# A fixed TensorE order in the attention, scores and weights of exactly 128 columns, and two query blocks' scores in one PSUM bank

## The chip, the core and the metric

The kernel runs on one core of a Trainium2 chip. A core has a matrix engine (TensorE, PE in the profile; its weight loads are listed as PEld), a vector engine (VectorE, DVE), a scalar engine (ScalarE, ACT), a general engine (GpSimd, POOL) and a queue engine that here starts the loads (SyncE, SP). Each engine works through its own queue in order, and an instruction waits on semaphores that other engines raise. TensorE writes its results to PSUM, a small memory of eight banks, each of which holds 512 float32 columns on 128 partitions; the other engines read them there.

The metric is the device time of one execution in microseconds (us). The kernel before was run three times, 884.99, 886.83 and 887.63 us, with the median 886.83.

## The reference

One block of a streaming encoder, for 512 frames of 1024 features, in float32:

```python
xn = rmsnorm(h, norm_mix_g[l])
u = jnp.einsum('bsd,de->bse', xn, w_in[l])
q, k, v, xr, gr, ga, gb = jnp.split(u, splits, axis=-1)
ya = chunked_band_attention(q, k, v, rel_table[l]) @ w_attn_out[l]
...
h = h + (g_a * ya + g_b * yb) @ w_o[l]
...
h = h + (jax.nn.silu(g) * up) @ w_ffn_out[l]
```

The second branch `yb` is a causal convolution, a gated linear recurrence and a projection. The attention is what the change touches. It has 16 heads of 64 features. Frames lie in chunks of 64; a frame reads its own chunk and the eight chunks before it, and since there are only eight chunks, that is every chunk up to its own. A learned bias by clipped distance is added to the scores, then softmax, then the weighted sum of the values:

```python
s = jnp.einsum('bnqhd,bnkhd->bhnqk', q, kb).astype(jnp.float32) * scale
s = s + rel_bias_band(rel_table).astype(jnp.float32)[None, :, None, :, :]
...
p = jax.nn.softmax(s, axis=-1).astype(v.dtype)
o = jnp.einsum('bhnqk,bnkhd->bnqhd', p, vb)
```

## The kernel before

**Numbers in two parts.** Every float32 operand of a matmul is split into a high part, rounded to the type `float32r`, and the rest. ACT makes the high part and DVE the rest (`split`, lines 78 to 81). A full product takes three matmuls (`mm3`, lines 74 to 76): high by high, high by low, low by high. Weights arrive by loads on SP's queue (line 149), 512 KB at a time, and are split before use; in the profile these tiles are called `raw_..` and `whl_..`.

**Stages.** Norm and transposes, then the projections of the recurrent branch with its scan, then the attention, then the output projections (`ya`, `wo`), and the feed-forward part. In the time line the attention stands between about 235 and 448 us.

**The attention.** For a pair of heads `q_tile` and `k_tile` make q and k by 24 matmuls of 512 columns each, and evict them with ACT and DVE; `v_tile` makes a block of v for four heads with 24 matmuls of 256 columns. One head then has four steps.

- `scores(h)`, lines 638 to 659: the 512 queries are four blocks of 128. Query block `qb` reads the first `(qb + 1) * 128` keys. Two matmuls (lines 651 and 652) make its scores; both parts of q lie in one stationary operand, against the high and the low part of k. The matmuls are never under 256 columns wide: block 0 computes 256 and uses 128. The scores of blocks 0, 1 and 3 go to a PSUM tag `s` of two banks, those of block 2 to a tag `mm` of four. DVE adds the bias and finds the row's maximum in one instruction, followed by a short read-out into `m` (both at line 654); ACT takes the exponential and the row sum (line 655); DVE makes the reciprocals of the sums (line 656); POOL scales the four blocks (line 658). The bias tile of the head is loaded by SP and masked by POOL (lines 424 and 425).
- `transposed(h)`, lines 661 to 673: ten transposes on PE (line 670) turn the probabilities so that keys lie on partitions. Three PSUM tiles receive them, and ACT and DVE split them into tiles `pp`. The third `pp` holds key blocks 2 and 3; key block 3 has only 128 columns of queries, and 128 columns of zeros are set before it by POOL (line 664), so that its part is 256 wide. It is split in two pieces, of 256 and 128 columns.
- `weigh(h)`, lines 679 to 698: eight matmuls (line 690) of 512, 512, 384, 384, 256, 256, 256 and 256 columns add up the weighted values in one PSUM tile, which ACT and DVE evict.
- `laid(h)`, lines 702 to 711, names the projections that are put into the turn of head `h`, before or after its weighing: q and k tiles of later pairs, v blocks of the next group, and for heads 12 to 15 a gate projection each. Turns 4, 8 and 12 to 15 have one tile of 512 columns and nothing else.

**What sets the order.** The program is written out in the turns of lines 722 to 731: the transposes of head `h`, the scores of head `h + 1`, the projections before, the weighing, the projections after. The scores of head 0 are made earlier, among the projections `yb` (line 718). But the written order is not the order of the engines: the kernel is built with a scheduler (line 984) that puts the instructions of each engine into an order of its own, by a simulated time line. In the order it made, the scores of a head are often parted, with the fourth or third block many matmuls behind the others, and a weighing is mixed with scores or transposes of other heads. Waits are then set between the engines, where one instruction reads what another wrote or writes where another still reads.

Of the kernel before, what the change touches and what calls it, by code (L numbers as in the profile page):

```python
# [8 lines left out]
F32 = mybir.dt.float32  # L9
# [5 lines left out]
P = 128  # L15
D = 1024
S = 512
KT = D // P
NT = S // P
HEADS = 16  # L20
# [16 lines left out]
def block_kernel(ctx: ExitStack, tc: tile.TileContext, x, norm_mix_g, w_in, b_merge, rel_table,  # L37
# [3 lines left out]
    pe, dve, act, pool, sp = nc.tensor, nc.vector, nc.scalar, nc.gpsimd, nc.sync  # L41
# [21 lines left out]
    ps = ctx.enter_context(tc.tile_pool(name="ps", bufs=2, space=PSUM))  # L63
    dr = ctx.enter_context(tc.tile_pool(name="dr", bufs=1, space=bass.MemoryType.DRAM))

    def f(ap):
        return ap.bitcast(F32)

    def mm_tile(name, tag="mm"):
        return ps.tile([P, S], F32, tag=tag, bufs=4 if tag == "mm" else 2, name=name)  # L70
# [7 lines left out]
    def split(hi, lo, src):  # L78

        act.activation(hi, src, AF.Copy)  # L80
        dve.tensor_sub(lo, src, f(hi))  # L81
# [280 lines left out]
    def features(pl, tag, name):  # L362

        t = pl.tile([P, KT, 2, S], F32R, tag=tag, name=name)
        return t, [t[:, k] for k in range(KT)]
# [13 lines left out]
    _, xnT = features(xnp, "xn", "xnT")  # L379
# [40 lines left out]
    def bias_tile(h):  # L420
        b = aw.tile([P, S], F32, tag="bias", bufs=2, name=f"bias{h}")
        src = ext_d[h:h + 1, 0:S]
        band = bass.AP(tensor=src.tensor, offset=src.offset, ap=[[1, P], [1, S]])
        sp.dma_start(out=b[:], in_=band)
        pool.memset(b[64:128, 448:512], NEG)
        return b
# [150 lines left out]
    def blocks(ap):  # L577
        return ap.rearrange("p (b i) -> p b i", i=P)

    def backwards(ap):  # L580
        return blocks(ap)[:, :, ::-1]

    def halves(e):
        own, other = slice(e * HD, e * HD + HD), slice(HD - e * HD, 2 * HD - e * HD)
        return own, other
# [7 lines left out]
    def q_tile(pr):  # L593
        po = mm_tile(f"po_q{pr}")
        project(po, weights(f"qk{pr}"), 0, xnT)
        q = qk_pool(pr).tile([P, 2, S], F32R, tag="qk", bufs=3, name=f"q{pr}")
        for e in range(2):
            own, other = halves(e)
            src = backwards(po[own, :])
            act.activation(blocks(q[own, e]), src, AF.Copy, scale=0.125)  # L600
            dve.scalar_tensor_tensor(blocks(q[other, e]), src, 0.125, blocks(f(q[own, e])), ALU.mult, ALU.subtract)
        qk[pr] = [q]

    def k_tile(pr):
        po = mm_tile(f"po_k{pr}")
        project(po, weights(f"qk{pr}"), 1, xnT)
        kh = qk_pool(pr).tile([P, 2, S], F32R, tag="qk", bufs=3, name=f"kh{pr}")
        kl = qk_pool(pr).tile([P, 2, S], F32R, tag="qk", bufs=3, name=f"kl{pr}")
        for e in range(2):
            own, other = halves(e)  # L610
            act.activation(kh[own, e], po[own, :], AF.Copy)
            dve.tensor_sub(kl[own, e], po[own, :], f(kh[own, e]))
            act.activation(kh[other, e], po[own, :], AF.Copy)
            pool.tensor_copy(kl[other, e], kl[own, e])
        qk[pr] += [kh, kl]
# [11 lines left out]
    def v_tile(gr, t):  # L627
        wv = weights(f"v{gr}")
        po = mm_tile(f"po_v{gr}_{t}", "mm" if gr else "t")
        for k in range(KT):  # L630
            mm3(po[:, 0:256], xnT[k][:, 0, t * P:(t + 1) * P], xnT[k][:, 1, t * P:(t + 1) * P],
                wv(0, k, whole), wv(1, k, whole), k == 0, k == KT - 1)
        v = aw.tile([P, 2, 4, HD], F32R, tag="v", bufs=8, name=f"v{gr}_{t}")
        split(v[:, :, 0::3], v[:, :, 1:3], po[:, 0:256].rearrange("p (a b d) -> p a b d", a=2, b=2))
        vs.setdefault(gr, []).append(v)


    def scores(h):
        pr, e = divmod(h, 2)
        q, kh, kl = qk[pr]  # L640
        bias = bias_tile(h)
        lsum = cp.tile([P, NT], F32, tag="lsum", bufs=2, name=f"l{h}")
        nmax = cp.tile([P, NT], F32, tag="nmax", bufs=2, name=f"m{h}")
        rl = cp.tile([P, NT], F32, tag="rl", bufs=2, name=f"rl{h}")
        prob = [aw2.tile([P, (qb + 1) * P], F32, tag=f"p{qb}", name=f"p{h}_{qb}") for qb in range(NT)]
        for qb in range(NT):
            w = (qb + 1) * P
            wm = max(w, 256)
            sc = mm_tile(f"s{h}_{qb}") if qb == 2 else ps.tile([P, S], F32, tag="s", bufs=2, name=f"s{h}_{qb}")
            qs = q[:, e, qb * P:(qb + 1) * P]  # L650
            pe.matmul(sc[:, 0:wm], qs, kh[:, e, 0:wm], start=True, stop=False)
            pe.matmul(sc[:, 0:wm], qs, kl[:, e, 0:wm], start=False, stop=True)  # L652

            dve.tensor_tensor_reduce(prob[qb][:], sc[:, 0:w], bias[:, S - w:S], -1.0, 3e38, ALU.add, ALU.min, nmax[:, qb:qb + 1])  # L654
            act.activation(prob[qb][:], prob[qb][:], AF.Exp, bias=nmax[:, qb:qb + 1], scale=-1.0, accum_out=lsum[:, qb:qb + 1])  # L655
        dve.reciprocal(rl[:], lsum[:])  # L656
        for qb in range(NT):
            pool.tensor_scalar(prob[qb][:], prob[qb][:], rl[:, qb:qb + 1], 1.0, ALU.mult, ALU.mult)  # L658
        return prob

    def transposed(h, prob):

        pp = [aw2.tile([P, 2, S], F32R, tag="pt", bufs=4, name=f"pp{h}_{i}") for i in range(3)]
        pool.memset(f(pp[2][:, :, 256:384]), 0.0)
        for i, kbs in enumerate(((0,), (1,), (2, 3))):
            pt = mm_tile(f"pT{h}_{i}") if i == 2 else ps.tile([P, S], F32, tag="t", bufs=2, name=f"pT{h}_{i}")
            for kb in kbs:
                for qb in range(kb, NT):
                    at = qb - min(kb, 2) if kb < 3 else 2
                    pe.transpose(pt[:, at * P:(at + 1) * P], prob[qb][:, kb * P:(kb + 1) * P], ident[:])  # L670
            for at, lo, n in (((0, 0, 512),), ((0, 0, 384),), ((0, 0, 256), (384, 256, 128)))[i]:
                split(pp[i][:, 0, at:at + n], pp[i][:, 1, at:at + n], pt[:, lo:lo + n])
        return pp

    aT = []
# [3 lines left out]
    def weigh(h, pp):  # L679
        pr, e = divmod(h, 2)  # L680
        own, other = halves(e)
        if e == 0:
            oacc.append(tg_.tile([P, S], F32, tag="tg", name=f"oacc{pr}"))
        acc = oacc[pr]
        po = mm_tile(f"o{h}")
        for kb in range(NT):
            i, lo, n = ((0, 0, 512), (1, 0, 384), (2, 0, 256), (2, 256, 256))[kb]
            st = vs[pr // 2][kb][:, pr % 2, 2 * e:2 * e + 2].rearrange("p a d -> p (a d)")
            for part in range(2):
                pe.matmul(po[:, S - n:S], st, pp[i][:, part, lo:lo + n], start=kb == 0 and part == 0, stop=kb == NT - 1 and part == 1)  # L690
        act.activation(acc[own, :], po[other, :], AF.Copy)
        dve.tensor_add(acc[own, :], po[own, :], acc[own, :])
        if e == 1:
            if pr % 2 == 0:
                aT_pairs.append(rnp.tile([P, 2, 2, S], F32R, tag="big", bufs=4, name=f"aT{pr}"))
            o = aT_pairs[-1][:, pr % 2]
            split(blocks(o[:, 0]), blocks(o[:, 1]), backwards(acc[:]))
            aT.append(o)
# [3 lines left out]
    def laid(h):  # L702
        m, at = divmod(h, 4)
        qs, ks, va = (lambda pr: lambda: q_tile(pr)), (lambda pr: lambda: k_tile(pr)), (lambda t: lambda: v_tile(m + 1, t))
        if h >= 12:
            return [lambda: gate(0, h - 8)], []
        first_, second = 2 * m + 2, 2 * m + 3
        return {0: (([qs(1), ks(1)] if m == 0 else []) + ([] if m == 0 else [qs(first_)]), [qs(first_)] if m == 0 else []),
                1: ([ks(first_)], [va(0)]),
                2: ([va(1), va(2)], [va(3)]),  # L710
                3: ([qs(second)], [ks(second)])}[at]
# [4 lines left out]
    for j in range(KT):  # L716
        if j == 6:
            prob = scores(0)
        po = mm_tile(f"po_yb{j}")
        project(po, weights(f"yb{j - j % 2}"), j % 2, rnn)  # L720
        dve.scalar_tensor_tensor(zB[j], zB[j], 1.0, po[:], ALU.add, ALU.mult)
    for h in range(HEADS):
        pp = transposed(h, prob)
        if h + 1 < HEADS:
            prob = scores(h + 1)
        before, after = laid(h)
        for what in before:
            what()
        weigh(h, pp)
        for what in after:  # L730
            what()
    aw2_stack.close()
    wo_stack, wop = opened("wo", 4)
    extra["wo1"] = wop
# [3 lines left out]
    _, mT = features(xnp, "xn", "mT")  # L738
# [113 lines left out]
    sc_stack, sc = opened("sc", 2)  # L852
# [101 lines left out]
    for i, ((t, at), po) in enumerate(zip(pieces, pos)):  # L954
        for k0, wf in zip(ks[late:], wfs):
            out_tile(t, po, k0, wf, at)
        n = 1 + i // 4
# [30 lines left out]
```

## Time and profile before

| | |
|---|---|
| median of three runs | 886.83 us |
| the profiled execution's own time | 887.36 us |
| its span, first to last instruction | 885.6 us |
| mean granted TensorE clock | 0.997 |
| TensorE busy | 873.6 us, 99% of the span |
| weight loads busy | 778.1 us, 88% |
| DVE busy | 551.7 us, 62% |
| ACT busy | 472.6 us, 53% |
| POOL busy | 111.4 us, 13% |

The busy time of PE is that of overlapping matmuls: a matmul's record reaches past the start of the next one. What a matmul costs in a row of matmuls is therefore read from start to start, not from its length. The profile's other views are groups of instructions (line, engine, operation, written tile <- read tiles, shapes, count, then busy time and mean length in ns of one, then the idle time of the engine ahead of them and who ended it), the waits (who waited for whom: us in total, times, the longest), the time line (start, length, engine, line, operation, and in brackets the idle time before it), and the busy time of each engine by stretch with the granted clock.

### The profile page before, as it was taken

The page shows a single profiled execution, that of the slowest core. Times are in us where ns is not written, and L with a number is a line of the kernel's source. Part 1 is how long each engine was busy: PE and PEld are TensorE (multiplying, and loading weights), DVE is VectorE, ACT ScalarE, POOL GpSimd, SP SyncE. Part 2 cuts the span into 40 slices and gives each one's busy share as a digit, 9 for nine tenths or more (in the row PEclk, how much of TensorE's full clock was granted, in tenths as well). Part 3 has the DMA queues.
Part 4 walks back from the last instruction along what each step waited for, and adds up shares of the span by engine and source line. Part 5 has one row for each costly group of instructions (what it writes and reads, how often), then busy time and mean ns, then how long its engine had stood idle before and what let it go on. Part 6 is the DMA issues. An engine that isn't in the chain of part 4 may idle for free.

```text
span 885.6 us, 13331 instructions
## 1 busy us (share of the span) xinstructions
PE 873.6 (99%) x5220; PEld 778.1 (88%) x5220; DVE 551.7 (62%) x872; ACT 472.6 (53%) x839; POOL 111.4 (13%) x157
## 2 busy tenths in 40 slices
PE   8999999999999999999999999999999999999997
PEld 5988888888888989898888889999999999888886
DVE  5776557663456475765556556888878887553203
ACT  7566646652256485766633366656555555723203
POOL 4013111220022232222100000000000001300100
PEclk9999999999999999999999999999999999999999
DMA  8223233433333233232223720524333332353002
GB/s 266 86 82 104 86 95 94 122 95 95 97 96 93 61 96 96 72 108 72 62 84 121 258 75 22 165 74 126 113 95 96 100 128 84 119 180 126 27 1 95
DMA packets 86080, 90.10 MB, mean 102 GB/s; under 512 B 5377, under 2 KB 74609, under 8 KB 86017
## 3 DMA queue, kind: packets, MB, share of 16 engines
q1 hardware_dynamic: 84640, 85.78, 31.6%
q10 hardware_dynamic: 1376, 3.47, 1.0%
q8 instruction: 41, 0.67, 0.3%
q14 instruction: 23, 0.18, 0.1%
HBM read 87.10 MB, written 2.14 MB: 101 GB/s over the span
## 4 chain that ended last, share of the span: by engine, by line
PE 96%; DVE 2%; DMA 1%; ACT 1%; issue 0%; POOL 0%; ACTq 0%; DVEq 0%
PE po_out L75 5%; PE po_out L74 5%; PE po_out L76 5%; PE o L690 2%; PE p_fg L74 2%; PE p_fg L76 2%; PE p_fu L76 2%; PE p_fg L75 2%; PE p_fu L75 2%; PE p_fu L74 2%; PE pT L670 2%; PE po_v L74 2%; PE po_v L75 2%; PE po_v L76 2%; PE po_ga L74 2%; PE po_ga L75 2%
## 5 line engine op out<-in xcount | busy, mean ns | idle before, releaser
L75 PE MATMUL po_out<-whl_fo,act_hi 128*128 128x512 f32 (+1 forms) x198 | 72.5, 366 | 0.0
L74 PE MATMUL po_out<-whl_fo,act_hi 128*128 128x512 f32 (+1 forms) x198 | 72.3, 366 | 0.0
L76 PE MATMUL po_out<-whl_fo,act_lo 128*128 128x512 f32 (+1 forms) x198 | 71.7, 365 | 0.0
L81 DVE TENSOR_TENSOR whl_fo<-raw_fo,whl_fo 128x1024 fp32r<-128x1024 f32 x22 | 27.9, 1274 | 44.2 <-ACT whl_fo L80 43.8
L872 POOL TENSOR_TENSOR act_lo<-act,act_hi 128x1024 fp32r<-128x1024 f32 x4 | 10.9, 2718 | 325.2 <-ACT act_hi L871 323.2
L80 ACT ACTIVATE whl_fo<-raw_fo 128x1024 fp32r<-128x1024 f32 x22 | 23.0, 1057 | 49.0 <-PE po_out L76 35.4
L658 POOL TENSOR_SCALAR p<-p,rl 128x128 f32<-128x128 f32 (+1 forms) x64 | 35.1, 567 | 105.8 <-DVE rl L656 105.5
L655 ACT ACTIVATE p<-p,m 128x128 f32<-128x128 f32 (+2 forms) x64 | 35.7, 561 | 13.3 <-DVE m L654 12.9
L74 PEld LDWEIGHTS po_out<-whl_fo,act_hi 128*128 128x128 f32 x198 | 37.4, 189 | 6.1
L76 PEld LDWEIGHTS po_out<-whl_fo,act_lo 128*128 128x128 f32 x198 | 37.3, 189 | 6.0
L75 PEld LDWEIGHTS po_out<-whl_fo,act_hi 128*128 128x128 f32 x198 | 37.4, 189 | 5.9
L74 PE MATMUL po_v<-whl_v,xnT 128*128 128x256 f32 x128 | 36.7, 287 | 0.0
L75 PE MATMUL po_v<-whl_v,xnT 128*128 128x256 f32 x128 | 36.5, 285 | 0.0
L76 PE MATMUL po_v<-whl_v,xnT 128*128 128x256 f32 x128 | 36.5, 285 | 0.0
L654 DVE CUSTOM_DVE_ANT_0 p<-s,bias 128x128 f32<-128x128 f32 (+2 forms) x64 | 30.2, 487 | 8.8 <-PE s L652 8.1
L81 DVE TENSOR_TENSOR pp<-pT,pp 128x256 fp32r<-128x256 f32 (+2 forms) x64 | 29.1, 486 | 3.4 <-ACT pp L80 3.0
L75 PE MATMUL po_xr<-xnT,whl_xr 128*128 128x512 f32 (+1 forms) x80 | 27.9, 354 | 0.6 <-DVE xnT L358 0.6
L81 DVE TENSOR_TENSOR whl_fg_s<-s_fg,whl_fg_s 128x1024 fp32r<-128x1024 f32 x20 | 25.6, 1294 | 3.7 <-ACT whl_fg_s L80 3.7
L74 PE MATMUL po_gr<-xnT,whl_gr 128*128 128x512 f32 (+1 forms) x80 | 27.8, 349 | 0.1
L81 DVE TENSOR_TENSOR whl_qk<-raw_qk,whl_qk 128x1024 fp32r<-128x1024 f32 x16 | 20.0, 1250 | 12.5 <-ACT whl_qk L80 11.9
L76 PE MATMUL po_gr<-xnT,whl_gr 128*128 128x512 f32 (+1 forms) x80 | 27.5, 348 | 0.3 <-DVE whl_gr L81 0.3
L75 PE MATMUL po_gr<-xnT,whl_gr 128*128 128x512 f32 (+1 forms) x80 | 27.6, 346 | 0.0
(348 smaller groups left out, 3062.0 us busy)
## 6 DMA issues: line engine op xcount, KB each, us to landing
raw_fg<-in_w_ffn_in_dram SPq DMA_DIRECT2D x24, 512.0 KB, 4.5
raw_fu<-in_w_ffn_in_dram SPq DMA_DIRECT2D x22, 512.0 KB, 4.1
raw_fo<-in_w_ffn_out_dram SPq DMA_DIRECT2D x22, 512.0 KB, 4.3
raw_qk<-in_w_in_dram SPq DMA_DIRECT2D x32, 256.0 KB, 3.3
raw_xr<-in_w_in_dram SPq DMA_DIRECT2D x8, 512.0 KB, 4.5
raw_gr<-in_w_in_dram SPq DMA_DIRECT2D x8, 512.0 KB, 3.5
raw_ga<-in_w_in_dram SPq DMA_DIRECT2D x8, 512.0 KB, 3.6
raw_gb<-in_w_in_dram SPq DMA_DIRECT2D x8, 512.0 KB, 3.5
```

The lines of the kernel that those rows point to most:

```text
L74: pe.matmul(o, sh, mh, start=start, stop=False, skip_group_check=parts)
L75: pe.matmul(o, sh, ml, start=False, stop=False, skip_group_check=parts)
L76: pe.matmul(o, sl, mh, start=False, stop=stop, skip_group_check=parts)
L80: act.activation(hi, src, AF.Copy)
L81: dve.tensor_sub(lo, src, f(hi))
L654: dve.tensor_tensor_reduce(prob[qb][:], sc[:, 0:w], bias[:, S - w:S], -1.0, 3e38, ALU.add, ALU.min, nmax[:, qb:qb + 1])
L655: act.activation(prob[qb][:], prob[qb][:], AF.Exp, bias=nmax[:, qb:qb + 1], scale=-1.0, accum_out=lsum[:, qb:qb + 1])
L658: pool.tensor_scalar(prob[qb][:], prob[qb][:], rl[:, qb:qb + 1], 1.0, ALU.mult, ALU.mult)
L670: pe.transpose(pt[:, at * P:(at + 1) * P], prob[qb][:, kb * P:(kb + 1) * P], ident[:])
L690: pe.matmul(po[:, S - n:S], st, pp[i][:, part, lo:lo + n], start=kb == 0 and part == 0, stop=kb == NT - 1 and part == 1)
L872: (pool if i in (0, 1, 2, 4) else dve).tensor_sub(lo[:], o[:], f(hi[:]))
```

## The change

Four edits, all in the attention.

1. Each query block's scores are exactly as wide as its keys: block 0 now has 128 columns.
2. The scores of blocks 0 and 1 share one PSUM tile of the tag `s`, in columns 0 to 127 and 256 to 511. Block 3 has the other bank of that tag to itself.
3. Key block 3 of the transposed probabilities is no longer padded with zeros: the POOL memset is gone, the third `pp` is split in one piece of 384 columns instead of two of 256 and 128, and the last two weighing matmuls have 128 columns.
4. The head loop stands in a manual schedule for TensorE: within it, PE's instructions keep the written order. The other engines are still ordered by the scheduler.

```diff
         for qb in range(NT):
             w = (qb + 1) * P
-            wm = max(w, 256)
-            sc = mm_tile(f"s{h}_{qb}") if qb == 2 else ps.tile([P, S], F32, tag="s", bufs=2, name=f"s{h}_{qb}")
+
+            if qb != 1:
+                bank = mm_tile(f"s{h}_{qb}") if qb == 2 else ps.tile([P, S], F32, tag="s", bufs=2, name=f"s{h}_{qb}")
+            sc = bank[:, 256:512] if qb == 1 else bank
             qs = q[:, e, qb * P:(qb + 1) * P]
-            pe.matmul(sc[:, 0:wm], qs, kh[:, e, 0:wm], start=True, stop=False)
-            pe.matmul(sc[:, 0:wm], qs, kl[:, e, 0:wm], start=False, stop=True)
+            pe.matmul(sc[:, 0:w], qs, kh[:, e, 0:w], start=True, stop=False, skip_group_check=qb < 2)
+            pe.matmul(sc[:, 0:w], qs, kl[:, e, 0:w], start=False, stop=True, skip_group_check=qb < 2)
...
-        pool.memset(f(pp[2][:, :, 256:384]), 0.0)
...
-            for at, lo, n in (((0, 0, 512),), ((0, 0, 384),), ((0, 0, 256), (384, 256, 128)))[i]:
-                split(pp[i][:, 0, at:at + n], pp[i][:, 1, at:at + n], pt[:, lo:lo + n])
+            n = (512, 384, 384)[i]
+            split(pp[i][:, 0, 0:n], pp[i][:, 1, 0:n], pt[:, 0:n])
...
-            i, lo, n = ((0, 0, 512), (1, 0, 384), (2, 0, 256), (2, 256, 256))[kb]
+            i, lo, n = ((0, 0, 512), (1, 0, 384), (2, 0, 256), (2, 256, 128))[kb]
...
-    for h in range(HEADS):
-        pp = transposed(h, prob)
-        if h + 1 < HEADS:
-            prob = scores(h + 1)
-        before, after = laid(h)
-        for what in before:
-            what()
-        weigh(h, pp)
-        for what in after:
-            what()
+    with tc.manual_schedule(engines={mybir.EngineType.PE}):
+        for h in range(HEADS):
+            pp = transposed(h, prob)
+            if h + 1 < HEADS:
+                prob = scores(h + 1)
+            before, after = laid(h)
+            for what in before:
+                what()
+            weigh(h, pp)
+            for what in after:
+                what()
```

In the changed kernel the lines from 646 on move by up to two: scores are at 653 and 654, the reduction and its read-out at 656, transposes at 671, the weighing at 691.

## The prediction

> **What bounds the kernel now.** I read the busy times first, then the chain that ended last, then busy time by stretch around the attention, and last the waits of TensorE.
>
> ```profile
> PE 873.6 (99%) x5220; PEld 778.1 (88%) x5220; DVE 551.7 (62%) x872; ACT 472.6 (53%) x839; POOL 111.4 (13%) x157
> ...
> PE 96%; DVE 2%; DMA 1%; ACT 1%; issue 0%; POOL 0%; ACTq 0%; DVEq 0%
> ```
>
> TensorE (PE) is busy 99% and is 96% of the chain. So a microsecond of matmul work added or removed, and each microsecond in which PE waits, goes into the time one for one; work on the other engines counts only where PE waits for it.
>
> ```profile
> 235.00:448.00 213.00, 211.39 (x1214) 186.81 (x1214) 133.31 (x303) 133.96 (x301) 52.07 (x107) 0.99 0.31 87
> ...
> 280.00:284.00 4.00, 2.39 (x14) 1.53 (x13) 2.68 (x7) 2.23 (x6) 2.73 (x6) 0.96 0.49 142
> 284.00:288.00 4.00, 4.00 (x24) 4.00 (x23) 2.49 (x8) 2.84 (x10) 0.77 (x2) 0.62 0.33 66
> 448.00:880.00 432.00, 430.66 (x2857) 397.62 (x2855) 274.82 (x373) 206.08 (x351) 16.89 (x8) 1.00 0.32 104
> ```
>
> Columns: stretch, length, busy PE, PEld, DVE, ACT, POOL, then the granted clock. The attention (235 to 448) holds 1.6 us of PE idle in 213, all of it between 280 and 284; then the clock fell: (1 - 0.96) x 4 + (1 - 0.62) x 4 = 1.7 us lost, that is 3.4 us at half speed. DVE is busy 133 of 213, 63%.
>
> The waits of PE and of its weight loads name the cause of that one hole, and the timeline shows it:
>
> ```profile
> PE pT L670 <- POOL p L658: 1.4, 1, 1.4
> ```
> ```profile
> PEld pT L670 <- POOL p L658: 2.5, 3, 1.8
> ```
> ```profile
> 280.47 0.40 PE L652 MATMUL s<-kl,q 128*128 128x512 f32 x1
> 282.22 1.56 PE L670 MATMUL pT<-ident,p 128*128 128x128 f32 x6 [1.36 <-POOL p L658]
> ```
> ```profile
> 282.67 0.20 PEld L670 LDWEIGHTS pT<-ident,p 128*128 128x128 f32 x2 [0.32 <-POOL p L658]
> 283.23 0.31 PEld L670 LDWEIGHTS pT<-ident,p 128*128 128x128 f32 x3 [0.36 <-POOL p L658]
> ```
>
> The transposes of head 2 came up before its probabilities were scaled: 282.22 - 280.47 less the matmul's own slot of 0.23 is 1.52, and 0.32 + 0.36 follow: 2.2 us. With the clock's 1.7 this hole costs 3.9 us.
>
> **Part 1, the shared bank.** Query blocks 0 and 1 of a head now lie in one PSUM tile. In the changed kernel's instruction order the second block's matmul carries a wait:
>
> ```
> L671 Matmult pT_2<-ident,p_3 128x128 x2
> L653 Matmult s_0<-kh,q 128x128
> L654 Matmult s_0<-kl,q 128x128
> L653 Matmult s_0<-kh,q 128x256 [waits DVE_49]
> L654 Matmult s_0<-kl,q 128x256
> ```
>
> The count it waits for belongs to the read-out (m) of block 0's reduction of the same head: PE may write the bank again only when DVE has left it. Before, each block had its own bank and no wait on its own head. Held up behind it on PE is all that follows: blocks 2 and 3, the projections, the weighing. It holds for heads 1 to 15; head 0's scores stand outside the fixed order, and there the scheduler puts some 20 other matmuls between the blocks.
>
> The rows for its price:
>
> ```profile
> 275.71 0.28 PE L652 MATMUL s<-kl,q 128*128 128x256 f32 x1
> ...
> 275.83 1.45 PE L690 MATMUL o<-pp,v 128*128 128x512 f32 x8
> 276.03 0.29 DVE L654 CUSTOM_DVE_ANT_0 p<-s,bias 128x128 f32<-128x128 f32 x1 [0.21 <-PE s L652]
> ...
> 276.24 0.08 DVE L654 DVE_READ_ACCUMULATOR2_ANT m<- 128x1 f32 x1
> ```
> ```profile
> 564.04 0.38 ACT L275 ACTIVATE keepa_fg<-p_fg 128x256 f32<-128x256 f32 x1 [2.98 <-PE p_fg L76]
> ...
> 564.48 0.38 PE L74 MATMUL p_fg<-bt,whl_fg_s 128*128 128x256 f32 x1 [0.47 <-ACT keepa_fg L275]
> ...
> 564.70 0.28 PE L75 MATMUL p_fg<-bt,whl_fg_s 128*128 128x256 f32 x1
> ...
> 564.82 0.28 PE L76 MATMUL p_fg<-bt,whl_fg_s 128*128 128x256 f32 x1
> ```
>
> With DVE free: matmul to its end 0.28, DVE starts 0.04 later (276.03 after 275.99), reduction and read-out end 0.29 after that (276.32), PE resumes 0.06 after its releaser (564.48 after 564.42): 0.67, of which 0.12 would have passed anyway: 0.55. After such a wait the first matmul takes 0.22 to the next instead of 0.12: 0.10 more. So 0.65 at the least.
>
> What stands before that reduction in DVE's queue I read from the changed order, with these means:
>
> ```profile
> L81 DVE TENSOR_TENSOR whl_qk<-raw_qk,whl_qk 128x1024 fp32r<-128x1024 f32 x14 | 17.5, 1248 | 11.8 <-ACT whl_qk L80 11.1 <-DMA bias<-ext_d 0.7
> ...
> L655 ACT ACTIVATION_READ_ACCUMULATOR p<-p,m 128x1 f32 x64 | 12.3, 191 | 0.0
> ...
> L655 ACT ACTIVATE p<-p,m 128x512 f32<-128x512 f32 x16 | 11.5, 720 | 10.0 <-DVE m L654 9.8
> L658 POOL TENSOR_SCALAR p<-p,rl 128x512 f32<-128x512 f32 x16 | 11.1, 692 | 0.0
> L654 DVE CUSTOM_DVE_ANT_0 p<-s,bias 128x512 f32<-128x512 f32 x16 | 11.0, 688 | 4.5 <-PE s L652 4.3
> L81 DVE TENSOR_TENSOR pp<-pT,pp 128x512 fp32r<-128x512 f32 x16 | 11.0, 687 | 1.8 <-ACT pp L80 1.8
> ...
> L80 ACT ACTIVATE pp<-pT 128x512 fp32r<-128x512 f32 x16 | 9.5, 591 | 4.5 <-PE pT L670 4.5
> L658 POOL TENSOR_SCALAR p<-p,rl 128x384 f32<-128x384 f32 x16 | 9.4, 586 | 0.0
> ...
> L81 DVE TENSOR_TENSOR pp<-pT,pp 128x384 fp32r<-128x384 f32 x16 | 8.8, 550 | 0.0
> ...
> L600 ACT ACTIVATE q<-po_q 64x512 fp32r<-64x512 f32 x14 | 8.3, 592 | 11.2 <-PE po_q L76 8.1 <-DVE q L601 3.0
> L658 POOL TENSOR_SCALAR p<-p,rl 128x256 f32<-128x256 f32 x16 | 8.2, 511 | 0.0
> L658 POOL TENSOR_SCALAR p<-p,rl 128x128 f32<-128x128 f32 x16 | 7.7, 480 | 105.8 <-DVE rl L656 105.5
> ...
> L656 DVE RECIPROCAL rl<-l 128x4 f32<-128x4 f32 x16 | 2.8, 176 | 6.1 <-ACT p L655 5.8
> ```
>
> - Heads 3 to 5, 7 to 9, 11 to 13: only work whose inputs came earlier. At 63% busy DVE will now and then be mid-instruction, so I add 0.1: 9 x 0.75 = 6.8 us.
> - Heads 2, 6, 10, 14: the first split of the transposes (pp, 128x512) stands ahead. From the first transpose: fourth transpose's end 0.60 (three slots of 0.10 and its length), 0.04, ACT's copy 0.59, 0.03, DVE's split 0.69, reduction and read-out 0.29, wake 0.06: 2.30. Unhindered, PE would be there after ten transposes and two scores, 1.01 + 0.24 = 1.25. So 1.05, or 1.64 if ACT first ends a q eviction of 0.59; mean 1.35, and 0.10 to restart: 4 x 1.45 = 5.8.
> - Heads 1 and 15: a whole weight split (1.25) was just begun: 1.6 each with part of it left, 1.7 with the restart: 3.4.
>
> Together 16.0 us. The ends: 0.65 for all fifteen is 9.8; 1.74 for all six long ones and 0.75 for nine is 17.2. The Trainium skill (PSUM — Partial Sum Buffer, PSUM bank collisions raise a hardware error) says PSUM is to be guarded by bank and quadrant, not by address. By address block 1 would need no wait and the sum would lose these 16.0; the order shows the wait, so I go by the bank.
>
> **Part 2, 128 columns.** Per head two scores matmuls and two weighing matmuls go from 256 to 128 columns: 64 in all. No row has such a matmul. Slots from start to start:
>
> ```profile
> 275.14 0.39 PE L75 MATMUL po_k<-xnT,whl_qk 128*128 128x512 f32 x1
> ...
> 275.37 0.39 PE L76 MATMUL po_k<-xnT,whl_qk 128*128 128x512 f32 x1
> ...
> 277.12 0.28 PE L74 MATMUL po_v<-whl_v,xnT 128*128 128x256 f32 x1
> ...
> 277.24 0.28 PE L75 MATMUL po_v<-whl_v,xnT 128*128 128x256 f32 x1
> ...
> 277.36 0.28 PE L76 MATMUL po_v<-whl_v,xnT 128*128 128x256 f32 x1
> ```
> ```profile
> 380.19 1.25 PE L670 MATMUL pT<-ident,p 128*128 128x128 f32 x10
> 381.20 0.48 PE L651 MATMUL s<-kh,q 128*128 128x512 f32 x1
> ```
>
> 512 columns take 0.23, 256 take 0.12; the line through them gives 0.065 for 128: the low end, a gain of 64 x 0.055 = 3.5 us. Ten 128-column transposes take 1.01, so 0.10 each: narrow work leaves the line. The high end is the 512 row, a narrow matmul as dear as the widest: a loss of 64 x 0.11 = 7 us. Nearest are the same operation at 256 columns (0.12) and the transposes (0.10); I take 0.12, so nothing, and keep both ends.
>
> Gone with it: 16 POOL memsets and 16 pairs of 128-column splits on ACT and DVE. PE waits for none of them (the one wait of the profile is for p, not pp), so nothing.
>
> **Part 3, program order.** Each turn is now transposes(h), scores(h+1), projections, weighing(h), projections. Head 2's transposes now follow a whole k tile (24 x 0.23 = 5.5), a weighing (1.3, from 275.83 to 277.12) and a v tile (24 x 0.12 = 2.9) after its scores, 9.7 us, so the hole's 3.9 us go. What is late next is the turn with only one q tile or gate between (5.5 + 1.3 = 6.8 us: into heads 5, 9, 13, 14, 15). Behind the last score come 0.69 + 0.08 on DVE, 0.72 + 0.19 on ACT, 0.18, then four POOL scalings of 0.48 + 0.51 + 0.59 + 0.69: 4.1; with three splits ahead on DVE (0.69 + 0.55 + 0.55) 5.9, and wakes. It barely fits; I charge 0.5 us in all. For weighing, the splits have scores and a projection before them, 6.7 us. SP's queue and its loads follow the work and PE waits for none. Matmuls before 235 and after the attention keep their order.
>
> **The sum** goes against the profiled execution, 887.4 us (span 885.6): + 16.0 + 0 + 0.5 - 3.9 = 900.0. That run lies 0.5 above the median of the three, 886.8, so I forecast 899.4.
>
> **Rivals.** (a) Narrow matmuls fall to the 512 slot: + 7, less some 1.3 since in six heads the wait runs from the transposes and overlaps the longer slot: 905. For it: the transposes stand at 0.10, above the line. Against: no f32r row does it; at 256 columns it runs at 0.12. The Trainium skill (FP8 and Floating Point Precision, TensorE Precision Notes) gives true FP32 four passes; were that to hold for narrow f32r, the slot would be about 4 x 0.055 + 0.01 = 0.23, an estimate, the same end. No row here shows it.
>
> (b) The clock falls again. After 2.2 us of waits among transposes it stood at half for 3.4 us, costing 1.7. Six heads wait 1.0 to 1.7 us right after 1.0 us of transposes. Four of them throttled: + 6.8, 906. Against: 0.5 us holes (564) left the clock at 1.00. The Trainium skill (TensorE: Matmul & The Clock Gate, Why this matters for your kernels) warns of idle gaps over about 3 us; by that no head would throttle, though here 2.2 us sufficed.
>
> (c) The other side: block 1 finds DVE done, at line 653, so that the order's gain is left: 887.4 - 3.9 - 0.5 = 883.0, or 879.5 with the line's widths. It decides where the mean wait is under 3.9 / 15 = 0.26 us. Against: end of matmul, reduction and wakes alone leave 0.55.
>
> (d) All low ends at once: 887.4 + 9.8 - 3.9 - 3.5 - 0.5 = 889.3, no change that counts.
>
> **Chances.** Forecast (893 to 902.5) 0.53, (a) 0.30, (b) 0.09, (d) 0.05, (c) 0.03. A difference under 0.3%, 2.7 us, can't be told from none. So faster 0.03, same 0.05, slower 0.92. The range reaches from 893 (low widths, short waits) to 907, over (a) and most of (b).
>
> **What would show it.** PE idle of 13 to 16 us in the attention, put down to DVE m at line 656 before line 653, fifteen times, the longest in heads 2, 6, 10, 14, 1 and 15. The start distance of the 128-column matmuls at 653, 654 and 691 settles part 2; the clock by stretch settles (b); no wait for POOL at head 2 settles part 3. I am wrong if those waits are under 0.3 us, or if PE waits for p at many heads.

## The result and the profile after

The changed kernel takes 901.6 us (median of four runs, 901.54 to 903.84) where the kernel before, run beside it, takes 886.9 (four runs): a ratio of 1.0175, with a 95% interval from 1.0153 to 1.0197. The forecast was 899.4 in a range of 893 to 907. The profiled execution took 901.54 us, with a span of 899.8.

The busy times and the chain's shares by engine, from the page of the changed kernel:

```profile
PE 874.4 (97%) x5220; PEld 778.3 (87%) x5220; DVE 552.2 (61%) x856; ACT 472.0 (52%) x823; POOL 103.9 (12%) x141
...
PE 92%; DVE 4%; ACT 2%; issue 1%; DMA 1%; SPq 0%; DVEq 0%; ACTq 0%
```

PE has as much busy time as before (873.6) in a span 14 us longer, and DVE has 4% of the chain instead of 2%: PE waits for DVE. Where it does is seen in the busy time by stretch (columns as before):

```profile
235.00:464.00 229.00, 214.69 (x1221) 188.51 (x1220) 133.67 (x287) 133.18 (x285) 44.70 (x92) 0.99 0.28 81
464.00:894.00 430.00, 429.07 (x2851) 396.48 (x2849) 275.06 (x373) 206.28 (x351) 16.90 (x8) 1.00 0.33 104
374.00:378.00 4.00, 2.24 (x16) 2.04 (x15) 3.43 (x8) 2.92 (x7) 0.00 (x0) 0.94 0.00 0
378.00:382.00 4.00, 4.00 (x13) 3.13 (x12) 1.47 (x7) 2.02 (x6) 1.28 (x3) 0.63 0.21 65
```

The attention, now 235 to 464, has 14.3 us without PE; what comes behind it is full. Between 377 and 381 the clock stood at half: (1 - 0.94) x 4 + (1 - 0.63) x 4 = 1.7 us lost. PE's and its weight loads' waits in the attention all have one name:

```profile
PE s L653 <- DVE m L656: 14.3, 15, 1.8
```
```profile
PEld s L653 <- DVE m L656: 16.4, 15, 1.9
```

Fifteen waits, one at each head from 1 to 15, before block 1's first matmul (line 653), ended by the read-out (m) of block 0's reduction (line 656). No wait for POOL's p is left. From start to start, the time from block 0's second matmul to block 1's first, less the 0.11 that it takes without a wait, is in heads 1 to 15: 1.57, 1.23, 1.14, 0.66, 0.65, 1.93, 1.14, 0.66, 0.65, 1.93, 1.14, 0.66, 0.65, 1.12, 1.71, together 16.8 us. Each time the next matmul then starts 0.22 later instead of 0.12, so 0.10 more: 18.3 us in all.

Head 3 shows one of them. First PE, then DVE, from the time line of the changed kernel:

```profile
282.72 1.25 PE L671 MATMUL pT<-ident,p 128*128 128x128 f32 x10
283.73 0.30 PE L653 MATMUL s<-kh,q 128*128 128x128 f32 x1
283.87 0.28 PE L654 MATMUL s<-kl,q 128*128 128x128 f32 x1
285.12 0.38 PE L653 MATMUL s<-kh,q 128*128 128x256 f32 x1 [0.97 <-DVE m L656]
285.34 0.28 PE L654 MATMUL s<-kl,q 128*128 128x256 f32 x1
```
```profile
283.28 1.13 DVE L81 TENSOR_TENSOR aT<-oacc,aT 128x512 fp32r<-128x512 f32 x1
284.43 0.43 DVE L81 TENSOR_TENSOR v<-po_v,v 128x256 fp32r<-128x256 f32 x1
284.78 0.28 DVE L656 CUSTOM_DVE_ANT_0 p<-s,bias 128x128 f32<-128x128 f32 x1
284.98 0.08 DVE L656 DVE_READ_ACCUMULATOR2_ANT m<- 128x1 f32 x1
```

Block 0's scores end at 284.15; DVE is still at the split of aT (to 284.41), then at that of v, and begins the reduction at 284.78. The read-out ends at 285.06, and PE goes on 0.06 later.

### The profile page after: what moved, and what is told of

Read it like the earlier page. It is cut to its first block, busy times and chain, and to the rows that moved or that the text cites. A ratio compares the mean times of both kernels' runs of the same rounds, so it can differ in the third digit from the quotient of the medians.

```text
span 899.8 us, 13312 instructions
## 1 busy us (share of the span) xinstructions
PE 874.4 (97%) x5220; PEld 778.3 (87%) x5220; DVE 552.2 (61%) x856; ACT 472.0 (52%) x823; POOL 103.9 (12%) x141
## 4 chain that ended last, share of the span: by engine, by line
PE 92%; DVE 4%; ACT 2%; issue 1%; DMA 1%; SPq 0%; DVEq 0%; ACTq 0%
PE po_out L74 4%; PE po_out L76 4%; PE po_out L75 4%; PE p_fg L74 2%; PE p_fg L76 2%; PE p_fu L76 2%; PE p_fg L75 2%; PE p_fu L75 2%; PE p_fu L74 2%; PE o L691 2%; PE po_k L74 2%; PE po_k L76 2%; PE po_k L75 2%; PE po_ga L74 2%; PE po_q L74 2%; PE po_q L76 2%
## 5 line engine op out<-in xcount | busy, mean ns | idle before, releaser
L653 PE MATMUL s<-kh,q 128*128 128x128 f32 (+2 forms) x64 | 22.1, 357 | 14.3 <-DVE m L656 14.3
```

The source lines that it names most:

```text
L653: pe.matmul(sc[:, 0:w], qs, kh[:, e, 0:w], start=True, stop=False, skip_group_check=qb < 2)
```

## The experiments

My theory: the loss is made by two edits together. The shared bank puts a wait between block 0 and block 1, and the fixed order leaves nothing to do on PE between them. The rivals: the bank costs this much by itself; the fixed order does; the narrow matmuls do.

### One edit, or two, at a time

Three edits (bank, order, width) have eight combinations, and the six that were still missing were run. Each ratio is against the kernel before on the same chip.

| bank shared | order fixed | 128 columns | median us | ratio | interval |
|---|---|---|---|---|---|
| yes | | | 884.95 | 0.9983 | 0.9970 to 0.9996 |
| | yes | | 891.96 | 1.0060 | 1.0045 to 1.0075 |
| | | yes | 886.24 | 0.9997 | 0.9985 to 1.0010 |
| yes | | yes | 883.65 | 0.9974 | 0.9955 to 0.9993 |
| | yes | yes | 891.36 | 1.0051 | 1.0036 to 1.0066 |
| yes | yes | | 901.18 | 1.0163 | 1.0148 to 1.0178 |
| yes | yes | yes | 901.6 | 1.0175 | 1.0153 to 1.0197 |

**The bank alone** (the kernel before with blocks 0 and 1 in one bank):

```diff
-            sc = mm_tile(f"s{h}_{qb}") if qb == 2 else ps.tile([P, S], F32, tag="s", bufs=2, name=f"s{h}_{qb}")
+            if qb != 1:
+                bank = mm_tile(f"s{h}_{qb}") if qb == 2 else ps.tile([P, S], F32, tag="s", bufs=2, name=f"s{h}_{qb}")
+            sc = bank[:, 256:512] if qb == 1 else bank
...
```

> The kernel before with the shared bank alone: the scheduler's order and 256 columns stay. Theory A (the scheduler puts other matmuls between block 0 and block 1, so the bank costs nothing by itself; only together with the fixed order does it): 883 to 887, no wait of PE for m before block 1. Rival B (sharing a bank costs the handover wherever it is, 0.55 us at each head): 893 or more.

It is not slower; if anything it is 0.2% faster. Its weight loads wait for m nowhere in the attention; the one wait there is the old hole at head 2:

```profile
PEld pT L672 <- POOL p L660: 2.2, 2, 1.9
```

In its time line head 1 has blocks 2 and 3 and 22 projection matmuls, 6.0 us in all, between block 0 and block 1. So the bank costs nothing where the scheduler puts other matmuls between the blocks. Rival B is out. Why it is a little faster I have not found out.

**The order alone** (the kernel before with the head loop in the manual schedule):

```diff
-    for h in range(HEADS):
-        pp = transposed(h, prob)
+    with tc.manual_schedule(engines={mybir.EngineType.PE}):
+        for h in range(HEADS):
+            pp = transposed(h, prob)
...
```

> The kernel before with TensorE's fixed order alone; its banks and its 256 columns stay. Theory A (the fixed order costs by itself, because nothing is put between a head's score blocks any more and block 3 needs block 0's bank again): waits of PE for the reduction m before block 3's matmul at all fifteen heads, 9 us in the weight loads' row as with own banks and narrow matmuls, no wait for p at head 2; 891.4 and 64 narrow slots of 0.03 given up, 893. Rival B (the order alone is harmless and the earlier run with own banks lost its time to the narrow matmuls): at most 886, with no such waits.

5.4 us slower than the kernel before. The weight loads' waits in the attention:

```profile
PEld s L651 <- DVE m L654: 10.0, 15, 1.5
```

The hole at head 2 is gone, and fifteen new waits stand before block 3 (line 651 is its first matmul here). The tag s has two banks, for blocks 0, 1 and 3, so block 3 takes block 0's bank again and waits for the same reduction, only with 0.6 us of scores of blocks 1 and 2 between. From start to start these waits are 7.6 us, and 0.10 to restart fifteen times: 9.2; less the hole's 3.9, 5.3, against 5.4 measured. The fixed order thus exposes DVE's work even without the shared bank.

**The bank undone** (the changed kernel with own banks; order and widths stay):

```diff
-            if qb != 1:
-                bank = mm_tile(f"s{h}_{qb}") if qb == 2 else ps.tile([P, S], F32, tag="s", bufs=2, name=f"s{h}_{qb}")
-            sc = bank[:, 256:512] if qb == 1 else bank
+            sc = mm_tile(f"s{h}_{qb}") if qb == 2 else ps.tile([P, S], F32, tag="s", bufs=2, name=f"s{h}_{qb}")
```

> The changed kernel with the bank sharing undone: blocks 0, 1 and 3 of the scores take turns in the two banks as before; fixed order and 128 columns stay. Theory A (the wait of block 1 for block 0's reduction is the loss): the wait moves to block 3, which now reuses block 0's bank four matmuls (0.6 us) later, so each of the fifteen waits shrinks by 0.6: from 16.8 us in all to about 8; the time falls from 901.6 to about 892. Theory B (the fixed order makes TensorE late whatever the banks): no wait at block 1, but the waits turn up at the transposes or the weighing, and the time stays at 899 or more. Theory C (the narrow matmuls are dear): no change from the changed kernel, 901.

891.36, and the same waits at block 3:

```profile
PEld s L651 <- DVE m L654: 9.3, 15, 1.3
```

**The order undone** (the changed kernel without the manual schedule):

```diff
-    with tc.manual_schedule(engines={mybir.EngineType.PE}):
-        for h in range(HEADS):
-            pp = transposed(h, prob)
+    for h in range(HEADS):
+        pp = transposed(h, prob)
...
```

> The changed kernel without the fixed order: the scheduler orders TensorE again; the shared bank and 128 columns stay. Theory A: the scheduler puts other matmuls between block 0 and block 1, as it does for head 0, so most of the fifteen waits are covered: 883 to 889, by whether the hole at head 2's transposes (3.9 us) comes back. Theory B: back to the kernel before, 886 to 887, with no wait at block 1. Theory C: 901 or a little less.

883.65, a little faster than the kernel before. The hole at head 2 is back and shorter, and nothing else waits in the attention:

```profile
PEld pT L671 <- POOL p L660: 1.9, 2, 1.5
```

From the table, bank and order together cost 1.0163 - 1.0060 - (0.9983 - 1) = 0.0120, some 10.6 us, beyond what each does alone. That is the theory's point, in one number.

**The widths undone** (the changed kernel with 256 columns and the padding again) **and the widths alone** (the kernel before with 128):

```diff
+            wm = max(w, 256)
...
-            pe.matmul(sc[:, 0:w], qs, kh[:, e, 0:w], start=True, stop=False, skip_group_check=qb < 2)
-            pe.matmul(sc[:, 0:w], qs, kl[:, e, 0:w], start=False, stop=True, skip_group_check=qb < 2)
+            pe.matmul(sc[:, 0:wm], qs, kh[:, e, 0:wm], start=True, stop=False, skip_group_check=qb < 2)
+            pe.matmul(sc[:, 0:wm], qs, kl[:, e, 0:wm], start=False, stop=True, skip_group_check=qb < 2)
...
+        pool.memset(f(pp[2][:, :, 256:384]), 0.0)
...
-            i, lo, n = ((0, 0, 512), (1, 0, 384), (2, 0, 256), (2, 256, 128))[kb]
+            i, lo, n = ((0, 0, 512), (1, 0, 384), (2, 0, 256), (2, 256, 256))[kb]
```

> The changed kernel with the widths undone: block 0's scores 256 columns wide, the zero padding and the split in two pieces back; shared bank and fixed order stay. Theory A: 64 matmuls go from about 0.09 to 0.12 us each in the trace of the changed kernel, so about 2 us slower than it, 903.5; fifteen waits as before. Theory C: the narrow matmuls were the loss, so faster than the changed kernel, 895 or less.

901.18: no difference from the changed kernel, so the number missed, while rival (a) of the prediction, by which undoing the width would have gained 5.6 us (905 less 899.4), is out. The profile of this run had no half clock in the attention (the changed kernel's lost 1.7 us), and its waits, from start to start, add up to 16.4 us instead of 16.8: most of the longer ones shrink, since the longer matmul covers a little of them, while that of head 9 grew by 0.35. Both hide a gain of the narrow matmuls, which is itself smaller than the 2 us that Theory A took from their own slots (see Part 2 below).

> The kernel before with 128-column scores and weights alone; its banks and the scheduler's order stay. Theory A (a narrow matmul takes 0.03 us less of PE than one with 256 columns): 2 us under the kernel before, 884.5, with the wait for p at head 2 and perhaps its half clock; another 1.7 us less if the clock does not fall. Rival B (the width is worth nothing, and the shared bank is what made the scheduled variant faster): 886.4 with the hole as before. Rival C (narrow matmuls fall to the slot of 512 columns): 893.

886.24 against 886.61: unclear. Some of what the matmuls gain goes into the hole, since PE comes earlier to the same late probabilities: PE's own wait there is 2.2 us instead of 1.4. Some more goes at the matmul behind each narrow pair (see Part 2 below). How the two share it was not worked out. The weight loads' row, to be compared with 2.5 of before:

```profile
PEld pT L669 <- POOL p L658: 2.7, 2, 2.4
```

### Cover between block 0 and block 1

**Block 1 last.** The changed kernel with the score blocks in the order 0, 2, 3, 1, so that 0.8 us of other scores lie between the two that share a bank:

```diff
-        for qb in range(NT):
+        shared = None
+        for qb in (0, 2, 3, 1):
...
-            sc = bank[:, 256:512] if qb == 1 else bank
+            shared = bank if qb == 0 else shared
+            sc = shared[:, 256:512] if qb == 1 else bank
```

> The changed kernel with only the order of the score blocks changed: 0, 2, 3, 1, so that the four matmuls of blocks 2 and 3 (0.8 us) lie between block 0 and block 1; bank, widths and fixed order stay. Theory A: each of the fifteen waits shrinks by 0.8 us, to about 5.6 us in all with most short ones gone, and the time falls to 888 to 891. Theory B and C: 900 to 902, the order of blocks within a head matters to neither.

888.36 (ratio 1.0025, 1.0016 to 1.0034): 13 of the 15 us come back by order alone. The waits left, and a new one:

```profile
PEld s L655 <- DVE m L658: 6.4, 9, 1.1
...
PEld pT L673 <- POOL p L662: 1.5, 3, 0.5
```

Nine heads instead of fifteen, and heads 5, 9 and 13 now wait for their probabilities.

**The same with the widths undone**, by the edit shown above, of which the lines of the weighing again:

```diff
-            i, lo, n = ((0, 0, 512), (1, 0, 384), (2, 0, 256), (2, 256, 128))[kb]
+            i, lo, n = ((0, 0, 512), (1, 0, 384), (2, 0, 256), (2, 256, 256))[kb]
```

> The changed kernel with the score blocks in the order 0, 2, 3, 1, as in the run before, and its widths undone: 256 columns and the padding again. Hardly any wait and no fall of the clock is left to blur the price of the width. Theory A (0.03 us less for each of 64 narrow matmuls, less what the longer slots cover of the remaining waits): 889.5 to 890.5 against 888.4. Rival B (the width is worth nothing, as the earlier comparison of 901.2 with 901.6 said): 888.4. Rival C (narrow matmuls are dearer): under 887.

889.28 (1.0033, 1.0022 to 1.0044), 0.0008 or 0.7 us over the run before it, with intervals that overlap. In the table the width gives 0.0009 in both pairs with one of the other edits, 0.0003 with neither, and -0.0012 with both, and the intervals overlap each time. So the times do not prove a gain. From the first transpose to the first matmul behind the last weighing, the profiled run with 128 columns takes 195.9 us and the one with 256 takes 196.6: a gain of 0.7, well under the 2 us that the slots by themselves give.

**What stands ahead on DVE.** The changed kernel with the subtraction of the aT split given to POOL:

```diff
-            split(blocks(o[:, 0]), blocks(o[:, 1]), backwards(acc[:]))
+            act.activation(blocks(o[:, 0]), backwards(acc[:]), AF.Copy)
+            pool.tensor_sub(blocks(o[:, 1]), backwards(acc[:]), f(blocks(o[:, 0])))
```

> The changed kernel with the subtraction of each aT split (1.13 us on DVE, once per pair of heads) done by POOL instead; all else stays. Theory A (in heads 3, 7 and 11 block 0's reduction stood behind that split, which is why their waits were 1.14 us and not 0.65): those three fall to about 0.65, the other waits stay, the sum of waits falls by 1.5 us and the time to about 900. Rival B (something else sets those three, such as the v split or the scores' own length): they stay at 1.1 us.

In heads 3, 7 and 11 the wait is now 0.66 each, the others are as they were. Head 3 in the time line of this run, DVE and then PE:

```profile
283.57 0.42 DVE L81 TENSOR_TENSOR v<-po_v,v 128x256 fp32r<-128x256 f32 x1 [0.50 <-ACT v L80]
284.18 0.29 DVE L656 CUSTOM_DVE_ANT_0 p<-s,bias 128x128 f32<-128x128 f32 x1 [0.18 <-PE s L654]
```
```profile
283.77 0.28 PE L654 MATMUL s<-kl,q 128*128 128x128 f32 x1
284.53 0.38 PE L653 MATMUL s<-kh,q 128*128 128x256 f32 x1 [0.49 <-DVE m L656]
```

DVE is idle when the scores come. The profiled run took 898.45: the changed kernel's 901.54 less 1.4 of waits and less the 1.7 of the half clock, which did not come here, is 898.4. The kernel was run only twice, and the second run took 901.28 at a mean clock of 0.994 instead of 0.998. So the median, 899.87 (1.0148, 1.0111 to 1.0185), can't be told from the changed kernel's, and it is the waits that show the cause.

**Block 0 ahead of the transposes.** The changed kernel with block 0's scores of head h + 1 first, then the transposes of head h, then blocks 2, 3 and 1. Now 1.0 us of transposes and 0.9 of scores lie between the two:

```diff
-        for qb in range(NT):
+        shared = None
+        for qb in (0, 2, 3, 1):
+            if qb == 2:
+                yield prob
...
+            coming = scores(h + 1) if h + 1 < HEADS else None
+            if coming:
+                next(coming)
             pp = transposed(h, prob)
-            if h + 1 < HEADS:
-                prob = scores(h + 1)
+            if coming:
+                prob = next(coming)
```

> The changed kernel with block 0's scores of the next head put ahead of this head's transposes, and its blocks 2 and 3 ahead of block 1; the shared bank, the fixed order and the widths stay. Theory A (the loss is the time from block 0's matmul to its read-out on DVE, with nothing on PE to cover it): 1.0 us of transposes and 0.8 us of other scores now cover it, the waits before block 1 fall under 2 us in all, 881 to 884, faster than both. Rival B (what counts is DVE's queue as a whole, so that the wait only goes elsewhere, to block 3's bank or to the transposes' probabilities): 887 to 892 with waits of 5 us or more at other lines.

882.48 (0.9951, 0.9937 to 0.9966): 0.5% faster than the kernel before, and the fastest of all that were run. The attention, by busy time:

```profile
235.00:464.00 229.00, 229.00 (x1306) 202.22 (x1305) 144.82 (x303) 138.74 (x293) 48.81 (x92) 1.00 0.30 89
```

PE is busy in all of it, at the full clock, with the same shared bank, the same fixed order and the same work.

> The same kernel as the run with block 0's scores ahead of the transposes, once more, beside the one with its widths undone and on the same chip: 881.5 to 883, faster than the kernel before by 0.4 to 0.6%, without a wait in the attention.

881.99 (0.9949, 0.9929 to 0.9969), on another chip.

**That, with the widths undone**, by the same edit, of which the line of the padding:

```diff
+        pool.memset(f(pp[2][:, :, 256:384]), 0.0)
```

> The kernel with block 0's scores ahead of the transposes, with its widths undone: 256 columns and the padding again. PE has no wait left in the attention there, so the width's price shows by itself. Theory A (by start distances a narrow pair takes 0.17 us instead of 0.24: 32 pairs, 2.1 us): 884.6 against 882.5. Rival B (the width is worth nothing, as the earlier comparisons of the changed kernel and of the kernel before said): 882.5. Rival C (what is gained on PE is given back because the attention is bound by something else): between them, with idle time of PE in the attention.

890.9 (1.0050, 1.0034 to 1.0066), 8.9 us above the run beside it. No theory had that. Little of it is a price of columns: PE waits for probabilities in heads 5, 9 and 13.

```profile
PEld pT L677 <- POOL p L665: 6.3, 12, 1.1
```

POOL's time line says why, here ahead of head 5's transposes:

```profile
316.23 0.15 POOL L425 MEMSET bias<- 64x64 f32 x1 [6.47 <-DMA bias<-ext_d]
316.44 0.61 POOL L614 CAST kl<-kl 64x512 fp32r<-64x512 f32 x1
317.15 2.06 POOL L665 TENSOR_SCALAR p<-p,rl 128x128 f32<-128x128 f32 x4
```

And the same place without the padding:

```profile
313.14 0.61 POOL L614 CAST kl<-kl 64x512 fp32r<-64x512 f32 x1 [4.57 <-DVE kl L612]
313.85 2.05 POOL L664 TENSOR_SCALAR p<-p,rl 128x128 f32<-128x128 f32 x4
315.96 0.15 POOL L425 MEMSET bias<- 64x64 f32 x1
```

With the padding in the program, the scheduler put the masking of a later head's bias tile ahead of this head's scalings on POOL. It waits for the tile's load, with POOL idle for 6.5 us, and four scalings stand behind it. From block 0's second matmul to block 2's first, heads 5, 9 and 13 take 2.0, 1.8 and 2.4 us longer than in the run without the padding, 6.2 in all. From the first transpose to the first matmul behind the last weighing this profiled run takes 196.5 us and the one beside it 189.3. Of these 7.2, the waits leave 1.0 for the wider matmuls. Another 1.1 lies ahead of the attention: in this profiled run the granted clock was 0.93 between 8 and 12 us and 0.65 between 12 and 16, and 1.00 in the other. That the order on POOL differs is read from the trace; an order of POOL changed alone was not tried.

## Why the prediction came out right

**The bound** held: what PE waits for goes into the time one for one. Of the 14.2 us between the two profiled executions, 901.54 - 887.36, the waits are + 18.3, the hole - 3.9, the half clock + 1.7, and the narrow matmuls - 1.4 (below): + 14.7. The other - 0.5 is not placed.

**Part 1** had the mechanism right: place, releaser, and the count of fifteen. The runs add what the prediction left open: the wait costs something only because the fixed order keeps the blocks together. The bank alone is at 0.9983, and the order alone at 1.0060. The size was 16.0 and came out at 18.3. By its three terms:

- "Only work whose inputs came earlier", nine heads at 0.75. Six of them took 0.76 with the restart, but two errors met there: the wait itself was 0.66 and not 0.55, since DVE begins 0.14 behind the matmul's recorded end and not 0.04 as in the one row of before, and the 0.1 added for a DVE in mid-instruction did not occur. Head 4, PE and then DVE, in the time line of the changed kernel:

```profile
297.33 0.28 PE L654 MATMUL s<-kl,q 128*128 128x128 f32 x1
298.10 0.39 PE L653 MATMUL s<-kh,q 128*128 128x256 f32 x1 [0.49 <-DVE m L656]
```
```profile
297.75 0.29 DVE L656 CUSTOM_DVE_ANT_0 p<-s,bias 128x128 f32<-128x128 f32 x1 [0.15 <-issue]
```

  Heads 3, 7 and 11 took 1.24, and with them the term is 8.2 instead of 6.8. The split of aT ran when the scores ended, and a mean share of busy time stood in for one known instruction of 1.13 us that falls there every time. The run with that split on POOL showed it.
- The four heads with a split of the transposes ahead, at 1.45: 1.33 and 1.22 in heads 2 and 14, but 2.03 in heads 6 and 10, so 6.6 instead of 5.8. The prediction let one q eviction stand ahead of the copy on ACT. In heads 6 and 10 there were two instructions, as the turn before has only one projection tile, so that the last weighing is evicted here too. Head 6, from the time line of the changed kernel, on ACT and then on DVE and PE:

```profile
321.41 0.59 ACT L692 ACTIVATE oacc<-o 64x512 f32<-64x512 f32 x1 [0.61 <-PE o L691]
322.03 0.59 ACT L600 ACTIVATE q<-po_q 64x512 fp32r<-64x512 f32 x1
322.65 1.36 ACT L80 ACTIVATE pp<-pT 128x512 fp32r<-128x512 f32 x3
```
```profile
322.75 0.69 DVE L601 SCALAR_TENSOR_TENSOR q<-po_q,q 64x512 fp32r<-64x512 f32 x1
323.48 0.69 DVE L81 TENSOR_TENSOR pp<-pT,pp 128x512 fp32r<-128x512 f32 x1
324.08 0.28 DVE L656 CUSTOM_DVE_ANT_0 p<-s,bias 128x128 f32<-128x128 f32 x1
```
```profile
322.39 0.28 PE L654 MATMUL s<-kl,q 128*128 128x128 f32 x1
324.43 0.39 PE L653 MATMUL s<-kh,q 128*128 128x256 f32 x1 [1.76 <-DVE m L656]
```

- Heads 1 and 15 at 1.7: 1.67 and 1.81.

The bank as the unit of the wait held too: in the changed kernel block 1 never writes block 0's columns and waits fifteen times, as the Trainium skill (PSUM — Partial Sum Buffer, PSUM bank collisions raise a hardware error) would have it. That wait is set in the program; no run here shows what the chip would do without it. Nor do the runs tell the bank from the tile, since the two blocks share both.

**Part 2** was costed at nothing between - 3.5 and + 7, and rival (a) at the upper end had 0.30. The slots, in the time line of the kernel with block 0 first and then of the same with 256 columns:

```profile
267.61 0.22 PE L657 MATMUL s<-kh,q 128*128 128x128 f32 x1
267.67 0.28 PE L658 MATMUL s<-kl,q 128*128 128x128 f32 x1
267.78 1.28 PE L675 MATMUL pT<-ident,p 128*128 128x128 f32 x10
```
```profile
268.64 0.28 PE L658 MATMUL s<-kh,q 128*128 128x256 f32 x1
268.75 0.28 PE L659 MATMUL s<-kl,q 128*128 128x256 f32 x1
268.87 1.25 PE L677 MATMUL pT<-ident,p 128*128 128x128 f32 x10
```

A pair takes 0.17 instead of 0.23 to 0.24, so a narrow matmul 0.087, and not the 0.12 that was taken. The weighing pairs of the changed kernel have the same 0.17. Weighing gives 16 x 0.066 = 1.1 us. Of each scores pair only the first slot counts in the changed kernel, 0.14 behind the transposes (283.73 to 283.87 above) where with 256 columns it is 0.20 to 0.21:

```profile
283.53 0.36 PE L653 MATMUL s<-kh,q 128*128 128x256 f32 x1
283.74 0.28 PE L654 MATMUL s<-kl,q 128*128 128x256 f32 x1
```

Fifteen times 0.06 is 0.9, together 2.0. But the matmul that comes right behind a narrow pair takes longer. Here is the first projection matmul behind head 1's weighing, in the changed kernel and then with the widths undone:

```profile
279.80 0.33 PE L74 MATMUL po_v<-whl_v,xnT 128*128 128x256 f32 x1
279.97 0.28 PE L75 MATMUL po_v<-whl_v,xnT 128*128 128x256 f32 x1
```
```profile
279.65 0.28 PE L74 MATMUL po_v<-whl_v,xnT 128*128 128x256 f32 x1
279.76 0.28 PE L75 MATMUL po_v<-whl_v,xnT 128*128 128x256 f32 x1
```

It takes 0.17 instead of 0.12. Eleven weighings have such a projection behind them, at 0.05 each, and five have transposes, at 0.02: 0.6 of the 1.1 is paid back, and the width gains 1.4 and not 2.0. The choice that failed was the nearest row: the transposes' 0.10 was read as a floor for narrow work, and float32r matmuls of the same width go under it. Rival (a) is refuted: the scores and weights of 128 columns are cheaper, while the four passes of its estimate would be 0.23 each. That the splits and memsets taken away cost nothing agrees with the changed kernel, which waits for neither p nor pp; in the arrangement with block 0 first, their return did cost, by way of POOL's order.

**Part 3.** The hole's 3.9 us went, as said: no wait for p is left. The 0.5 us for late probabilities did not come, probably because PE, now held up earlier in each turn, comes to the transposes later. In the kernel with block 1 last, with less waiting, heads 5, 9 and 13 did wait, three of the five named.

**The rivals.** (b) came true in one place of the four that it had: after head 10's wait of 1.93 us the clock fell for 3.4 us, which cost 1.7. (c), a version that hides the wait, was put at 883.0; the kernel that does hide it took 882.5 and 882.0. (d) did not come.

That the forecast came within 2.2 us of the median is in part luck, because errors met. The waits were 2.3 too small and the half clock (1.7) was missing; against that stand 1.4 for narrow matmuls that are cheaper and 0.5 for late probabilities that did not come, together 2.1. The 0.5 that is not placed goes the other way, and the 0.6 that was taken off, because the profiled run of before lay over its median, does not apply to the changed kernel, whose profiled run lies on its median.

## What to carry to other kernels

A bank shared by two blocks, or taken again two blocks later, costs nothing as long as the writer has other work for the length of the reader's queue; fix the order and that cover must be put there by hand, here 1.9 us of transposes and scores for a wait of 0.65 to 1.9. Size such a wait head by head from the reader's queue at that moment, since an average share of its busy time hides the one long instruction that always stands ahead. After moving work on one engine, look at what the scheduler then does on the others: an instruction that waits for a load, put ahead of the work that the bound engine needs, cost more, by the account above, than the wider matmuls that came back with it.

## What the runs showed of the hardware

- A float32r matmul of 128 columns takes 0.087 us in a pair, less than a float32 transpose of the same width (0.10); 256 columns take 0.12, 512 take 0.23. The projection matmul right behind such a pair takes 0.05 more than behind a pair of 256 columns, so that most of the pair's gain of 0.066 is gone.
- A wait of PE of 1.93 us, behind 1.0 us of transposes and two short matmuls, halved the clock for 3.4 us in head 10 but not in head 6 with the same wait; nor did it in the profiled runs with the widths undone (waits up to 1.88) or with aT on POOL (1.93). The Trainium skill (TensorE: Matmul & The Clock Gate, Why this matters for your kernels) warns of gaps over about 3 us; in this case shorter ones sufficed at times. The hole at head 2 shows the same: it halved the clock in the profiled runs of the kernel before (PE idle for 1.36 us at one go in the time line, where head 10 shows 1.76), of the bank alone (1.50) and of the widths alone (2.19), but not in that of the changed kernel without the fixed order (1.10). What decides it stays open.
- With DVE free, the handover of a bank from PE to DVE and back left PE 0.66 us without work, and another 0.10 went before the matmuls ran at their pace again; both figures repeat to 0.01 at six heads.
